# FFN up product by Strassen's scheme, inner activations to DRAM, down product as a phase of its own

## The chip, the cores and the metric

The program runs on one core of one Trainium2 chip. The metric is the device time of one execution in microseconds (us). A core has five engines that run in parallel and each take their own instructions in order: PE (TensorE: matmuls, with PEld its weight loads), DVE (VectorE), ACT (ScalarE), POOL (GpSimd) and SP, whose queue starts most of the transfers (DMA). Matmul results land in PSUM, everything else lies in SBUF.

## What is computed

The kernel does one step of a two-layer decoder for 1024 prompt positions and 64 sample positions (8 batches of 8), 1088 tokens in all, with a width of 1024. Each layer mixes the positions and then applies a feed-forward block with a causal convolution of three taps, and each of the two is followed by a normalisation of the residual sum:

```python
def conv_ffn(x, buf, w_up, conv_w, conv_b, w_down):
    h = x @ w_up                                   # 1024 -> 2 * 2816
    h, new_buf = causal_dwconv(h, buf, conv_w, conv_b)
    return (jax.nn.silu(h[..., :D_FF]) * h[..., D_FF:]) @ w_down, new_buf
...
x = layer_norm(ALPHA * x + mix, ...)
y, buf = conv_ffn(x, ...)
x = layer_norm(ALPHA * x + y, ...)
```

Only the feed-forward block, called FFN here, is changed. It runs twice, once per layer.

## The kernel before

Products are made nearly in float32: every operand is split into a high part and the rest (`split`, line 211: ACT rounds a copy, DVE subtracts it from the original), and `mm3` (line 202) makes three matmuls, high by high, high by low and low by high, for each product.

**The FFN** (`ffn`, line 255). The 2 x 2816 inner rows are taken in 22 blocks of 128 + 128 rows (gate and value). `up(blk)` loads and splits both weight blocks (`load_split`, 512 KB each) and goes through the tokens in three tiles of 364 columns; for each tile and half it makes 8 x 3 matmuls into one PSUM bank. ACT applies the middle tap (line 298), DVE adds the other two taps straight from PSUM (line 302), ACT applies SiLU, DVE multiplies (line 317) and the result is split again into `act`. `down(blks)` multiplies two blocks' activations by their rows of the down weights, 9 token tiles by two halves of 512 columns, and DVE adds each PSUM bank to the residual `res` in SBUF (line 352). `ffn` runs the up product two blocks ahead of the down product, so that PE has both kinds of work in turn. POOL has two small copies per block (lines 308, 314).

**Around it.** `out_ln` (line 1366) makes the residual sum and normalises it tile by tile; `to_T` (line 241) transposes each tile on PE and splits it into `x_`, which `ffn` reads. After the last `down` the loop `ffn_ln` (line 380) normalises the nine tiles while the last products run. In layer 0 the projection `in1` (line 1450) follows, in layer 1 the program ends. `run` (line 2201) calls them in turn.

**Storage and order.** SBUF is cut into fields A to G (`epoch`, `upper`); a field changes its type as a whole, and only when everything in it is done. Outside the attention stages the order on each engine is made by a scheduler when the program is built; at run time every engine keeps that order, and an instruction that waits holds up those behind it. In the traces the scheduled instructions have the line of the helper that records them.

Of the kernel before, what the change touches and what calls it, by code (L numbers as in the profile page):

```python
# [15 lines left out]
ALU = mybir.AluOpType  # L16
# [15 lines left out]
FIELDS = dict(A=8704, B=8704, C=9216, D=8768, F=8368)  # L32
TILES = ((0, 364), (364, 362), (726, 362))

# [37 lines left out]
class Group:  # L72
    """storage that is given back together"""
# [4 lines left out]
    def __call__(self, field, *shape):  # L78
        n = math.prod(shape)
        m = (n + 1) // 2 * 2  # L80
        top, field = field[-1] == "^", field.rstrip("^")
        field = next((f for f in field if f in self.net.arenas and self.net.arenas[f].fits(m)), field[0])
# [20 lines left out]
class Halves(tuple):  # L103
    """high and low parts; both: the two as one"""


class Net:
    token_tiles = (8, 0, 1, 2, 3, 4, 5, 6, 7)

    def __init__(self, ctx, tc, A):  # L110
# [7 lines left out]
        for f, t in zip("ABCDF", (F32R, F32R, F32, F32, F32)):  # L118
            self.epoch(f, t)
# [12 lines left out]
    # ---- storage: fields of SBUF, each of one type at a time, and banks of PSUM by use  # L132
# [8 lines left out]
    def upper(self, **fields):  # L141
        """cut the uppermost storage into these fields"""
# [52 lines left out]
    def stack(self, v, rows):  # L195
        """v [128, 2, 4, (hi, lo)]: both parts of the sample group side by side, for each row block"""
# [5 lines left out]
    def mm3(self, out, wh, wl, xh, xl, first, last):  # L202
        mm = self.nc.tensor.matmul
        mm(out, wh, xh, start=first, stop=False)  # L204
        mm(out, wh, xl, start=False, stop=False)  # L205
        mm(out, wl, xh, start=False, stop=last)  # L206
# [8 lines left out]
    def load_split(self, hi, lo, raw, src, eng=None):  # L215
        """src (DRAM, float32) by way of raw as its high and low parts"""
# [24 lines left out]
    def to_T(self, x, M, x_, c0):  # L241
        """x [M, 128 k] -> columns c0.. of the high and low parts x_: for each four k their [128, k, .]"""
# [11 lines left out]
    # ---- the feed-forward block: res <- ALPHA res + ffn(x)  # L254
    def ffn(self, i, x_, res):
        nc, A = self.nc, self.A
        g = self.group()
        raws = [g("F", D) for _ in range(4)]
        cpar = g("F", 2 * NBLK, 4)
        nc.sync.dma_start(cpar, A["ffn_cp"][i])  # L260
        stt = g("F", 2 * NBLK, NB, 2)
        nc.sync.dma_start(stt, A["ffn_st"][i])
        ffp = g("F", 2 * NBLK, 2)
        wu = [g("EG", 2, D) for _ in range(2)]
        wd = [g("EG", 2, D) for _ in range(2)]
        # a block's rows of all tokens: high parts, low parts of the sample group, of the prompt
        act = [g("D", 2 * NT) for _ in range(4)]
        high, low = (lambda a, c0, c1: a[:, c0:c1]), (lambda a, c0, c1: a[:, NT + NS + c0 : NT + NS + c1])
        nc.gpsimd.memset(res[NS:, NTT - 1, :], 0.0)
        cc = [g("F", 2, 364) for _ in range(2)]  # L270
        pr_ = g("F", D)
        pr = [pr_[:, 364 * k : 364 * k + 364] for k in range(2)]
        hh = [g("F", NB, 10) for _ in range(2)]
        cnt = dict(c=0, h=0)

        def up(blk):
            ws = []
            for half in range(2):
                w = wu[half]
                self.load_split(w[:, 0, :], w[:, 1, :], raws[half], A["w_up"][i, half * NBLK + blk])  # L280
                ws.append(w.rearrange("p s (k c) -> p s k c", k=8))
            a = act[blk % 4]
            for n in range(3):
                c0 = (0, 362, 724)[n]
                c, prod = cc[cnt["c"] % 2], pr[cnt["c"] % 2]
                cnt["c"] += 1
                wid = 364 if n == 0 else 362
                o0 = 364 - wid
                np_ = 298 if n == 2 else wid
                for half in range(2):  # L290
                    cb = half * NBLK + blk
                    w = ws[half]
                    ps = self.ps("mm")[:, :364]
                    for k in range(8):
                        xh, xl = (v[:, k % 4, c0 : c0 + 364] for v in x_[k // 4])
                        self.mm3(ps, w[:, 0, k, :], w[:, 1, k, :], xh, xl, k == 0, k == 7)
                    o = c[:, half, :]
                    nc.scalar.activation(o[:, :wid], ps[:, o0:], AF.Identity, bias=cpar[:, cb, 3:4], scale=cpar[:, cb, 2:3])  # L298
                    for tap, sh in ((1, 1), (0, 2)):
                        lo_ = max(0, sh - o0)  # L300
                        s0 = lo_ + o0 - sh
                        nc.vector.scalar_tensor_tensor(  # L302
                            o[:, lo_:np_], ps[:, s0 : s0 + np_ - lo_], cpar[:, cb, tap : tap + 1], o[:, lo_:np_], op0=ALU.mult, op1=ALU.add
                        )
                    if n == 2:
                        h = hh[cnt["h"] % 2]
                        cnt["h"] += 1
                        nc.gpsimd.tensor_copy(h[:, :, 0:2], stt[:, cb])
                        nc.scalar.copy(h[:, :, 2:10], ps[:, 300:].rearrange("p (b t) -> p b t", b=NB))
                        nc.scalar.copy(ffp[:, cb, :], ps[:, 298:300])  # L310
                        os = o[:, 298:362].rearrange("p (b t) -> p b t", b=NB)
                        for tap in (1, 0):
                            nc.vector.scalar_tensor_tensor(os, h[:, :, tap : tap + 8], cpar[:, cb, tap : tap + 1], os, op0=ALU.mult, op1=ALU.add)
                        nc.gpsimd.tensor_copy(stt[:, cb], h[:, :, 8:10])  # L314
                nc.scalar.activation(c[:, 0, :wid], c[:, 0, :wid], AF.Silu)
                t0 = (0, 364, 726)[n]
                nc.vector.tensor_tensor(prod[:, :wid], c[:, 0, :wid], c[:, 1, :wid], op=ALU.mult)
                nc.scalar.copy(a[:, t0 : t0 + wid], prod[:, :wid])
                if n < 2:
                    self.lo(low(a, t0, t0 + wid), prod[:, :wid], a[:, t0 : t0 + wid])  # L320
                else:
                    self.lo(low(a, t0, LP), prod[:, : LP - t0], a[:, t0:LP])
                    self.lo(a[:, NT : NT + NS], prod[:, LP - t0 : wid], a[:, LP:NT])

        def down(blks):
            ws = []
            for n, blk in enumerate(blks):
                # the last blocks take the place of the other weights
                w = (wd + wu)[n if len(blks) > 2 else blk % 2]
                self.load_split(w[:, 0, :], w[:, 1, :], raws[2 + blk % 2], A["w_dn"][i, blk])  # L330
                ws.append(w)
            def product(tt, pss, q):
                a_, b_ = tt * P, tt * P + P
                for nh in range(2):
                    cs, ps = slice(nh * 512, nh * 512 + 512), pss[nh]
                    for j in range(q, q + 2):
                        a, w = act[blks[j] % 4], ws[j]
                        first, last = j == 0, j == len(blks) - 1
                        if tt < 8:
                            self.mm3(ps, high(a, a_, b_), low(a, a_, b_), w[:, 0, cs], w[:, 1, cs], first, last)  # L340
                            continue
                        # both parts of the sample group at once, on 64 partitions each
                        for s in range(2):
                            nc.tensor.matmul(ps, a[:, LP : NT + NS], w[:, s, cs], start=first and s == 0, stop=last and s == 1)  # L344

            def add(tt, pss):
                for nh in range(2):
                    o = res[:, tt, nh * 512 : nh * 512 + 512]
                    if blks[0] == 0:
                        nc.vector.scalar_tensor_tensor(o, o, ALPHA, pss[nh], op0=ALU.mult, op1=ALU.add)  # L350
                    else:
# [1942 lines left out]
```

## Time and profile before

| | us |
|---|---|
| three runs | 3164.09, 3173.86, 3179.25 (median 3173.86) |
| span of the profiled execution, first to last instruction | 3159.4 |
| PE busy in the span | 3094.1 (98%) |
| DVE busy | 2127.2 (67%) |
| ACT busy | 1360.8 (43%) |
| POOL busy | 766.9 (24%) |

The profile gives no other time of its execution than the span. The difference between the span and the runs, 4.7 us for the fastest and 14.5 for the median, is what lies around it and how runs differ. A matmul's own duration in the rows is longer than the distance to the next one, since matmuls overlap; what one costs is read from the distance between starts.

### The profile page before, as it was taken

Reading aid. Unit: us, or ns where it says so; the run is one execution under the profiler, and the core shown is the slowest. Engines: PE = TensorE matmul, PEld = TensorE weight load, DVE = VectorE, ACT = ScalarE, POOL = GpSimd, SP = SyncE. Lnnn points to the kernel's source line nnn. Section 1 sums busy time; section 2 is a strip of 40 time slices with the busy share of each in tenths; the row PEclk is TensorE's granted clock in tenths of the full one; section 3 lists DMA queues with packets and bytes.
Section 4 is the critical chain, followed back from the end, with each engine's and each line's share of the span. In section 5 each row is a group of like instructions: output and inputs, shape, how many; then the busy total and the mean of one; then the engine's idle time right before and its main releaser. Section 6 shows DMA issues by size and latency. Waiting matters only on the chain.

```text
span 3159.4 us, 47267 instructions
## 1 busy us (share of the span) xinstructions
PE 3094.1 (98%) x18447; PEld 2797.6 (89%) x18447; DVE 2127.2 (67%) x3952; ACT 1360.8 (43%) x2527; POOL 766.9 (24%) x755
## 2 busy tenths in 40 slices
PE   8999999999999999999999999999999999999998
PEld 7888788999999999798998888888789999999997
DVE  8763648555555555747667999999685555555557
ACT  3434533322232232245555888888433222222221
POOL 3652520000000000201112999899200000000000
PEclk9998899999999999999999999999999999999999
DMA  3214131111111111310003444444511111111112
GB/s 138 79 47 122 53 131 56 52 43 41 41 48 46 41 47 43 108 36 23 31 28 103 165 167 156 178 158 167 202 57 41 54 41 41 41 53 42 41 41 75
DMA packets 83026, 243.02 MB, mean 77 GB/s; under 512 B 14908, under 2 KB 36604, under 8 KB 74484
## 3 DMA queue, kind: packets, MB, share of 16 engines
q1 hardware_dynamic: 71504, 154.98, 15.2%
q0 software_dynamic: 9216, 83.89, 7.4%
q8 instruction: 146, 2.39, 0.3%
q10 hardware_dynamic: 2084, 1.14, 0.1%
q14 instruction: 76, 0.62, 0.1%
HBM read 214.11 MB, written 24.68 MB: 76 GB/s over the span
## 4 chain that ended last, share of the span: by engine, by line
PE 82%; DVE 11%; ACT 4%; issue 2%; DMA 1%; POOL 1%; ACTq 0%; DVEq 0%; SPq 0%; POOLq 0%
PE ps L204 22%; PE ps L206 22%; PE ps L205 22%; DVE fieldF L2065 2%; DVE fieldD L209 2%; PE ps L2121 1%; PE ps L2011 1%; PE ps L344 1%; PE ps L2044 1%; DVE fieldF L2087 1%; DVE fieldB L209 1%; PE ps L1800 1%; PE ps L249 1%; PE ps L2025 1%; PE ps L1769 1%
## 5 line engine op out<-in xcount | busy, mean ns | idle before, releaser
L205 PE MATMUL ps<-fieldB,fieldE 128*128 128x364 f32 (+1 forms) x1488 | 494.5, 332 | 0.1
L302 DVE SCALAR_TENSOR_TENSOR fieldF<-ps,fieldF 128x362 f32<-128x362 f32 (+2 forms) x528 | 301.6, 571 | 284.7 <-ACT fieldF L298 275.7
L204 PE MATMUL ps<-fieldA,fieldE 128*128 128x364 f32 (+3 forms) x1440 | 477.0, 332 | 7.7 <-ACT fieldA L725 7.4
L206 PE MATMUL ps<-fieldA,fieldE 128*128 128x364 f32 (+3 forms) x1440 | 477.5, 332 | 0.0
L204 PE MATMUL ps<-fieldB,fieldE 128*128 128x364 f32 (+1 forms) x1104 | 365.4, 331 | 0.0
L206 PE MATMUL ps<-fieldB,fieldE 128*128 128x364 f32 (+1 forms) x1104 | 364.0, 330 | 0.0
L314 POOL COPY fieldF<-fieldF 128x16 f32<-128x16 f32 x88 | 17.4, 198 | 1399.9 <-ACT fieldF L310 1348.0
L205 PE MATMUL ps<-fieldA,fieldE 128*128 128x364 f32 x1056 | 347.2, 329 | 0.0
L352 DVE TENSOR_TENSOR fieldC<-fieldC,ps 128x512 f32<-128x512 f32 x324 | 222.2, 686 | 165.8 <-PE ps L206 163.6
L205 PEld LDWEIGHTS ps<-fieldB,fieldE 128*128 128x128 f32 x1488 | 283.8, 191 | 1.3 <-DVE fieldB L726 0.5
L204 PEld LDWEIGHTS ps<-fieldA,fieldE 128*128 128x128 f32 x1440 | 273.6, 190 | 9.9 <-ACT fieldA L725 7.4
L206 PEld LDWEIGHTS ps<-fieldA,fieldE 128*128 128x128 f32 x1440 | 273.8, 190 | 2.1 <-issue 0.9
L298 ACT ACTIVATE fieldF<-ps,fieldF 128x362 f32<-128x362 f32 (+1 forms) x264 | 172.5, 653 | 200.4 <-PE ps L206 200.4
L218 ACT CAST fieldE<-fieldF 128x1024 fp32r<-128x1024 f32 (+2 forms) x144 | 136.5, 958 | 280.9 <-PE ps L206 170.9
L219 DVE TENSOR_TENSOR fieldE<-fieldF,fieldE 128x1024 fp32r<-128x1024 f32 (+1 forms) x140 | 156.4, 1127 | 92.8 <-ACT fieldE L218 77.5
L204 PEld LDWEIGHTS ps<-fieldB,fieldE 128*128 128x128 f32 x1104 | 208.7, 189 | 0.9 <-issue 0.7
L206 PEld LDWEIGHTS ps<-fieldB,fieldE 128*128 128x128 f32 x1104 | 208.3, 189 | 0.1
L205 PEld LDWEIGHTS ps<-fieldA,fieldE 128*128 128x128 f32 x1056 | 198.6, 188 | 1.7
L204 PE MATMUL ps<-fieldE,fieldD 128*128 128x512 f32 (+1 forms) x480 | 187.4, 391 | 0.0
L205 PE MATMUL ps<-fieldE,fieldD 128*128 128x512 f32 (+1 forms) x480 | 185.6, 387 | 0.0
L206 PE MATMUL ps<-fieldE,fieldD 128*128 128x512 f32 (+1 forms) x480 | 185.4, 387 | 0.0
L209 DVE TENSOR_TENSOR fieldD<-ps,fieldE 128x1024 fp32r<-128x1024 f32 x128 | 153.9, 1209 | 0.6 <-ACT fieldE L2015 0.4
(596 smaller groups left out, 7289.3 us busy)
## 6 DMA issues: line engine op xcount, KB each, us to landing
fieldF<-w_up SPq DMA_DIRECT2D x88, 512.0 KB, 3.5
fieldF<-w_dn SPq DMA_DIRECT2D x44, 512.0 KB, 4.0
fieldF<-w_in SPq DMA_DIRECT2D x16, 512.0 KB, 4.0
fieldF<-w_out SPq DMA_DIRECT2D x32, 256.0 KB, 2.9
fieldC<-x_T SPq DMA_DIRECT2D x8, 544.0 KB, 7.0
fieldC<-x_tok SPq DMA_DIRECT2D x8, 512.0 KB, 6.3
xs<-fieldC SPq DMA_DIRECT2D x8, 512.0 KB, 2.6
Od<-fieldF SPq DMA_DIRECT2D x32, 128.0 KB, 1.7
```

The costliest lines, as they stand in the source:

```text
L204: mm(out, wh, xh, start=first, stop=False)
L205: mm(out, wh, xl, start=False, stop=False)
L206: mm(out, wl, xh, start=False, stop=last)
L209: self.nc.vector.tensor_tensor(out, full, hi, op=ALU.subtract)
L218: self.nc.scalar.copy(hi, raw)
L219: (eng or self.nc.vector).tensor_tensor(lo, raw, hi, op=ALU.subtract)
L249: nc.tensor.transpose(t[:, j * M : (j + 1) * M], x[:, (a + j) * P : (a + j + 1) * P], self.ident[:M, :M])
L298: nc.scalar.activation(o[:, :wid], ps[:, o0:], AF.Identity, bias=cpar[:, cb, 3:4], scale=cpar[:, cb, 2:3])
L302: nc.vector.scalar_tensor_tensor(o[:, lo_:np_], ps[:, s0 : s0 + np_ - lo_], cpar[:, cb, tap : tap + 1], o[:, lo_:np_], op0=ALU.mult, op1=A ...
L344: nc.tensor.matmul(ps, a[:, LP : NT + NS], w[:, s, cs], start=first and s == 0, stop=last and s == 1)
L352: nc.vector.tensor_tensor(o, o, pss[nh], op=ALU.add)
L2065: V.tensor_tensor_reduce(o, ps[H], o, op0=ALU.add, op1=ALU.max, accum_out=out[H], scale=1.0, scalar=first)
```

## The change

The rewritten `ffn` does three things.

**Strassen's scheme.** Weights and tokens are cut in halves: the weights' four blocks are the two halves of the contraction by gate and value rows, and the tokens are handled in two parts `u` of 544, each cut into 2 x 2 blocks of 512 contraction rows by 272 tokens. Instead of eight block products there are seven, P1 to P7 (`PRODUCTS`), each 4 x 3 matmuls with 272 columns. Their left factors are A11, A12, A22 and four sums S1 to S4 of weight blocks, made by POOL for every block of 128 rows (`sums`, and S4 in `weights`); their right factors are made once per FFN (`tokens`) and stay in fields A to E. Three of the products are added onto the PSUM bank of another. `taken` adds the products up into `R`, in SBUF; `conv` applies the taps from there, SiLU on ACT, the multiplication now on POOL.

**Activations to DRAM.** `conv` writes each block's product of gate and value to `actd` in DRAM, four DMAs per block.

**A down phase.** After all 22 blocks the tokens are taken in three groups of three tiles; for each, all 22 blocks of activations and down weights are loaded, split and multiplied, and the sums stay in six PSUM banks until the group ends. The residual comes from DRAM (`xm`, written by `out_ln`). The down weights are loaded three times. Normalisation of one group runs beside the next group's products; the last three blocks of the last group are done tile by tile.

```diff
+PRODUCTS = dict(P1=("A11", "B11"), P6=("S2", "T2"), P2=("A12", "B21"), P5=("S1", "T1"), P7=("S3", "T3"), P4=("A22", "T4"), P3=("S4", "B22"))
...
+        def tokens(u):
...
+            def parts(p, full, eng=V):
+                nc.scalar.copy(X[p][u][:, 0], full)
+                sub(eng, X[p][u][:, 1], full, X[p][u][:, 0])
+            parts("P1", B11)
+            parts("P2", B21)
+            sub(V, B11, B12, B11)
+            sub(G, B12, B22, B12)
+            parts("P3", B22, G)
+            sub(V, B22, B22, B11)
+            sub(V, B21, B21, B22)
+            parts("P6", B22)
+            parts("P5", B11)
+            parts("P7", B12, G)
+            parts("P4", B21)
...
+            G.tensor_tensor(S[0], A11, A21, op=ALU.subtract)
+            G.tensor_tensor(A21, A21, A22, op=ALU.add)
+            G.tensor_tensor(S[1], A21, A11, op=ALU.subtract)
...
+        def weights(p):
+            self.split(*W[p], self.left[PRODUCTS[p][0]])
+            if p == "P1":
+                G.tensor_tensor(self.left["S4"], self.left["A12"], self.left["S2"], op=ALU.subtract)
...
+            on = dict(P2="P1", P7="P6", P3="P5").get(p)
+            ps = bank[on or p, u]
+            x = X[p][u]
+            for k in range(4):
+                wh, wl = (w[:, k * P : k * P + P] for w in W[p])
+                self.mm3(ps, wh, wl, x[:, 0, k], x[:, 1, k], k == 0 and not on, k == 3, skip_group_check=on is not None)
...
+            if p == "P1":
+                nc.scalar.copy(s1, bank["P1", u])
+            elif p == "P2":
+                nc.scalar.copy(g_[:, h1], bank["P1", u])
+            elif p == "P6":
+                add(U2, s1, bank["P6", u])
+            elif p == "P7":
+                add(U3, s1, bank["P6", u])
+                add(v_[:, h2], U3, bank["P5", u])
+            elif p == "P4":
+                add(v_[:, h1], U3, bank["P4", u])
+            elif p == "P3":
+                add(g_[:, h2], U2, bank["P5", u])
...
+                nc.scalar.activation(y, x[:, 2:], AF.Identity, bias=c(3), scale=c(2))
+                for tap in (1, 0):
+                    V.scalar_tensor_tensor(y[:, :n], x[:, tap : tap + n], c(tap), y[:, :n], op0=ALU.mult, op1=ALU.add)
...
+            nc.scalar.activation(a, a, AF.Silu)
+            G.tensor_tensor(a, a, b, op=ALU.mult)
...
+                nc.sync.dma_start(d[:, at : at + c1 - c0], a[:, c0:c1])
...
+            for p in PRODUCTS if blk else first:
+                for u in range(2) if blk else (1,):
+                    product(p, u)
+                for u in range(2) if blk else (1,):
+                    taken(p, u)
+                if blk + 1 < NBLK:
+                    weights(p)
...
+            for u in range(2):
+                conv(blk, u)
...
+            nc.sync.dma_start(raw, actd[k][:, c0 : c0 + N])
+            self.load_split(w[:, 0], w[:, 1], wr[n % 2], A["w_dn"][i, k])
...
+        fetch(0, 0)
+        fetch(0, 1)
+        for u in range(2):
+            conv(NBLK - 1, u)
...
+            if n + 2 < len(todo):
+                fetch(*todo[n + 2])
...
+            for j in range(3):
+                product2(b, k, j)
```

`out_ln` writes each normalised tile to DRAM and `to_raw` leaves its transpose unsplit. `in1` keeps two buffers for its raw weights where it had four, and field F is now two fields, F and H.

**Places in the order of the instructions.** In rows of the order, `field...` are the SBUF fields, `ps...` the PSUM banks, then the columns.

DVE in the middle of an FFN, before (line 317 the product of gate and value, 209 and 219 splits, 302 taps read from PSUM, 313 taps of the sample group):

```order
L317 TENSOR_TENSOR fieldF5_67<-fieldF5_67 128x362
L209 TENSOR_TENSOR fieldD10_3695<-fieldF5_67,fieldD10_3695 128x362
L219 TENSOR_TENSOR fieldE7_71<-fieldF5_67,fieldE7_71 128x1024
L302 SCALAR_TENSOR_TENSOR fieldF5_67<-ps410_7346,fieldF5_67 128x298 x2
L313 SCALAR_TENSOR_TENSOR fieldF5_67<-fieldF5_67 128x64 x2
```

The same engine in the change, where one block ends and the next begins (380 and 390 are the taps of `conv`, 216 the weights' splits, 358 the additions in `taken`; the two rows with ps350 and ps351 take up P6 of the next block):

```order
L380 SCALAR_TENSOR_TENSOR fieldA10_2594<-fieldA10_2594,fieldF5_67 128x480
L390 SCALAR_TENSOR_TENSOR fieldA10_2594<-fieldA10_2594,fieldF5_67 128x64 x2
L216 TENSOR_TENSOR fieldH14_3847<-fieldA10_2594,fieldH14_3847 128x512
L390 SCALAR_TENSOR_TENSOR fieldA10_2594<-fieldA10_2594,fieldF5_67 128x64
L358 TENSOR_TENSOR fieldA10_2594<-fieldA10_2594,ps350_6987 128x272
L358 TENSOR_TENSOR fieldA10_2594<-fieldA10_2594,ps351_7000 128x272
L216 TENSOR_TENSOR fieldH14_3847<-fieldF5_67,fieldH14_3847 128x512
L216 TENSOR_TENSOR fieldH14_3847<-fieldA10_2594,fieldH14_3847 128x512 x2
```

The taps read their values from SBUF now, and the last taps of a block stand in front of the first additions of the next.

DVE in the change where `out_ln` ends and the FFN of layer 0 begins (245 and 246 the normalisation of the last tile, 301 the subtractions of `tokens`, 216 the weights' splits):

```order
L245 SCALAR_TENSOR_TENSOR fieldC12_3709<-fieldC12_3709,bmva0_7_4417,fieldF5_67 128x1024
L244 RECIPROCAL brsa0_7_4422<-brsa0_7_4422 128x1
L301 TENSOR_TENSOR fieldE16_4444<-fieldA10_2594,fieldE16_4444 128x1088
L246 SCALAR_TENSOR_TENSOR fieldC12_3709<-fieldC12_3709,brsa0_7_4422,fieldF5_67 128x1024
L216 TENSOR_TENSOR fieldH14_3847<-fieldF5_67,fieldH14_3847 128x512 x2
L216 TENSOR_TENSOR fieldE16_4444<-fieldF5_67,fieldE16_4444 128x512 x2
L301 TENSOR_TENSOR fieldC19_4450<-fieldA10_2594,fieldC19_4450 128x1088 x2
```

The parts of P1, the first product, lie in the new field C and so stand behind the last use of the old one. Thirteen more subtractions of that size follow on DVE, with a few additions between them; before, the first tile's matmuls stood directly behind the last product of `out_ln`.

SP's queue in the change, at the end of the up product (398 the writes of activations, 454 and 224 the loads of the down phase):

```order
L398 DMA act0_4451<-fieldA10_2594 128x256
L398 DMA act0_4451<-fieldA10_2594 128x288
L502 DMA fieldF5_67<-xm0_3711 64x1024
L398 DMA act0_4451<-fieldA10_2594 128x480
L398 DMA act0_4451<-fieldA10_2594 128x64
L454 DMA fieldF5_67<-act0_4451 128x320
L224 DMA fieldF5_67<-w_dn 128x1024
```

The loads of the first three blocks' activations stand ahead of these rows; the fourth block's stand behind the last block's writes.

## Rows read from the trace of the kernel before

**Rows 1.** The page: busy time by engine, and the span in 40 slices.

```profile
PE 3094.1 (98%) x18447; PEld 2797.6 (89%) x18447; DVE 2127.2 (67%) x3952; ACT 1360.8 (43%) x2527; POOL 766.9 (24%) x755
...
PE   8999999999999999999999999999999999999998
```

**Rows 2.** Chain of waits, two down tiles of layer 0: start us, us, what.

```profile
627.41 1.87 PE ps L344 x8
...
1278.37 1.88 PE ps L344 x8
```

**Rows 3.** Timeline of PE, first 364-column matmul of 25 in a row, and the last.

```profile
799.94 0.33 PE L205 MATMUL ps<-fieldB,fieldE 128*128 128x364 f32 x1
...
803.94 0.33 PE L205 MATMUL ps<-fieldB,fieldE 128*128 128x364 f32 x1
```

**Rows 4.** Timeline of PE, first 256-column matmul of ten in a row, and the last.

```profile
1479.20 0.28 PE L206 MATMUL ps<-fieldB 128*128 128x256 f32 x1
...
1480.27 0.28 PE L206 MATMUL ps<-fieldB 128*128 128x256 f32 x1
```

**Rows 5.** Groups by line and shape, DVE: busy us, mean ns | idle before.

```profile
L209 DVE TENSOR_TENSOR fieldB<-ps,fieldB 128x256 fp32r<-128x256 f32 x67 | 26.5, 420 | 22.0 <-ACT fieldB L1736 19.3 <-ACT fieldB L1811 1.8 <-PE ps L2011 0.9
L219 DVE TENSOR_TENSOR fieldE<-fieldF,fieldE 128x512 fp32r<-128x512 f32 x28 | 20.1, 738 | 3.3 <-issue 2.4 <-ACT fieldE L218 0.9
L238 DVE SCALAR_TENSOR_TENSOR fieldC<-fieldC,bmva,fieldF 128x1024 f32<-128x1024 f32 x16 | 20.5, 1279 | 0.4
L313 DVE SCALAR_TENSOR_TENSOR fieldF<-fieldF 128x64 f32<-128x64 f32 x176 | 51.4, 292 | 31.3 <-ACT fieldF L310 28.2
L726 DVE TENSOR_TENSOR fieldB<-fieldC,fieldA 128x1088 fp32r<-128x1088 f32 x8 | 10.3, 1291 | 0.9 <-ACT fieldA L725 0.7
```

**Rows 6.** The same, ACT.

```profile
L218 ACT CAST fieldE<-fieldF 128x512 fp32r<-128x512 f32 x28 | 16.7, 618 | 59.5 <-PE ps L1381 50.8 <-DMA fieldF<-w_out 8.4 <-PE ps L205 0.2
L725 ACT CAST fieldA<-fieldC 128x1088 fp32r<-128x1088 f32 x8 | 8.8, 1103 | 2.5 <-DMA fieldC<-x_T 2.5
L898 ACT COPY fieldD<-ps 128x272 f32<-128x272 f32 x16 | 5.8, 383 | 6.7 <-PE ps L891 6.5
```

**Rows 7.** Single lines of POOL: duration ns min/median/max, first and last start.

```profile
L1240 POOL TENSOR_TENSOR fieldG<-fieldG,fieldA x8: 1036/1045/1047, 329.3 to 408.6; 128x512 f32<-128x512 f32 x8
L1323 POOL TENSOR_TENSOR fieldD<-fieldD x4: 2488/2514/2703, 370.9 to 422.1; 128x1088 f32<-128x1088 f32 x4
L314 POOL COPY fieldF<-fieldF x88: 197/198/200, 555.1 to 3104.2; 128x16 f32<-128x16 f32 x88
```

**Rows 8.** One DVE line over all its runs, in the form of rows 7.

```profile
L2087 DVE SCALAR_TENSOR_TENSOR fieldF<-fieldF x64: 205/1298/2014, 1743.8 to 2242.6; 64x1 f32<-64x1 f32 x64
```

**Rows 9.** Timelines of DVE and of POOL around one of them.

```profile
1910.98 1.68 DVE L2087 SCALAR_TENSOR_TENSOR fieldF<-fieldF 64x1 f32<-64x1 f32 x1
...
1910.27 2.38 POOL L1997 TENSOR_TENSOR fieldB<-fieldA,fieldB 128x1024 fp32r<-128x1024 f32 x1
```

**Rows 10.** Timeline of PE where the first FFN follows `out_ln`.

```profile
529.16 0.39 PE L206 MATMUL ps<-fieldG,fieldD 128*128 128x512 f32 x1
529.39 0.33 PE L204 MATMUL ps<-fieldA,fieldE 128*128 128x364 f32 x1
```

**Rows 11.** Stretches after layer 0's FFN: busy us of PE, PEld, DVE, ACT, POOL, granted clock, DMA share, GB/s.

```profile
1330.00:1332.00 2.00, 0.00 (x0) 0.00 (x0) 2.00 (x3) 1.33 (x2) 2.00 (x1) 1.00 0.79 184
...
1334.00:1336.00 2.00, 1.17 (x5) 0.81 (x4) 0.69 (x1) 1.08 (x3) 2.00 (x2) 0.50 0.52 196
...
1344.00:1346.00 2.00, 2.00 (x17) 2.00 (x16) 1.72 (x3) 1.17 (x2) 0.00 (x0) 1.00 0.46 152
```

**Rows 12.** The end: the last matmul, and the last work of DVE.

```profile
3149.30 0.39 PE L206 MATMUL ps<-fieldE,fieldD 128*128 128x512 f32 x1
...
3154.59 1.28 DVE L239 SCALAR_TENSOR_TENSOR fieldC<-fieldC,brsf,fieldF 128x1024 f32<-128x1024 f32 x1
```

**Rows 13.** The page, DMA issues: KB each, us from issue to landing.

```profile
fieldF<-w_dn SPq DMA_DIRECT2D x44, 512.0 KB, 4.0
```

More of the change, by code (lines that the diff above doesn't have):

```diff
@@ L264, in ffn @@
[L264 to L274, printed above, removed]
@@ L325, in down @@
[L325 to L351, printed above, removed]
-                        nc.vector.tensor_tensor(o, o, pss[nh], op=ALU.add)
-            n = 2 if len(blks) > 2 else 0
-            some = {tt: [self.ps(("ac", "mm")[k]) for _ in range(2)] for k, tt in enumerate(self.token_tiles[:n])}
-            for tt, pss in some.items():
-                product(tt, pss, 0)
-            for tt in self.token_tiles:
-                pss = some.get(tt) or [self.ps("ac") for _ in range(2)]
-                for q in range(2 if tt in some else 0, len(blks), 2):
-                    product(tt, pss, q)
-                add(tt, pss)
@@ new lines, in load, with sums @@
+        def load(blk):
+            raw = raws[blk % len(raws)]
+            for half in range(2):
+                nc.sync.dma_start(raw[:, half * D : half * D + D], A["w_up"][i, half * NBLK + blk])
+        def sums(blk):
+            raw = raws[blk % len(raws)]
+            A11, A12, A21, A22 = (raw[:, k * 512 : k * 512 + 512] for k in range(4))
+            G.tensor_tensor(S[0], A11, A21, op=ALU.subtract)
+            G.tensor_tensor(A21, A21, A22, op=ALU.add)
+            G.tensor_tensor(S[1], A21, A11, op=ALU.subtract)
+            self.left = dict(A11=A11, A12=A12, A22=A22, S1=A21, S2=S[1], S3=S[0], S4=A11)
@@ new lines, in ffn @@
+        first = ("P1", "P2", "P6", "P5", "P7", "P4", "P3")
+        load(0)
+        sums(0)
+        for p in first:
+            weights(p)
+        tokens(0)
+        gt[0].free()
+        xf = "AD"[i]
+        R = [[gr(xf, 2 + HT) for _ in range(2)] for _ in range(2)]
+        U = [[gr(xf, QT) for _ in range(3)] for _ in range(2)]
+        hh = [gr(xf, NB, 2 + LS) for _ in range(2)]
+        for half in range(2):
+            G.memset(R[0][half][:, :2], 0.0)
+        for p in first:
+            product(p, 0)
+            taken(p, 0)
@@ new lines, in ffn @@
+        tokens(1)
+        gt[1].free()
+        o = [gr(xf, 2, HT) for _ in range(2)]
+        raws.append(gr(xf, 2 * D))
+        for blk in range(NBLK):
+            if blk + 1 < NBLK:
+                load(blk + 1)
+                sums(blk + 1)
+            for p in PRODUCTS if blk else first:
[3 more added lines that the diff above has]
+                    taken(p, u)
+                if blk + 1 < NBLK:
+                    weights(p)
+            if blk + 1 == NBLK:
+                break
+            for u in range(2):
+                conv(blk, u)
@@ L390, in ffn_ln @@
+        gl.free()
+        yield
+        for j in range(3):
+            for k in range(NBLK - 3, NBLK):
+                product2(2, k, j)
+            finish(2, j)
+        for j in range(3):
+            norm(2, j)
+            if j == 2:
+                g.free()
             yield
-        g.free()
 def lay(a):
@@ L1065, in ssd_decay @@
         gt.free()
-        rows = [bf(self.gd("F", 544), NT) for _ in range(2)]
+        rows = [bf(self.gd("HF", 544), NT) for _ in range(2)]
         for k, v in enumerate((cs, ec)):
@@ L1363, in mix0, with out_ln @@
         return [self.m0, m1]
-    def out_ln(self, name, i, m_, x_, res, src, ks=range(8), rows=None):
+    def out_ln(self, name, i, m_, XT, res, src, dst, ks=range(8), rows=None):
         nc, A = self.nc, self.A
@@ L1454, in in1 @@
         g = self.group()
-        raws = [g("F", 2, 352) for _ in range(4)]
+        gw = self.group()
+        raws = [gw("F", 2, 352) for _ in range(2)]
         ws = []
@@ L1854, in prompt_attention @@
         ot = [g("F^", 256) for _ in range(2)]
-        pb = [g("F^", LP) for _ in range(4)]
+        pb = [g("H^", LP) for _ in range(4)]
         mneg = g("F^", P)
@@ L2232, in run @@
         self.banks(mm=1, tr=2, ac=1)
-        gm, gt, gr = self.group(), self.group(), self.group()
+        gm, gt, gr, *gd = (self.group() for _ in range(5))
         heads = range(8)
@@ L2257, in run @@
         next(self.sample, None)
-        m_, res, rest = out
+        m_, XT, rest = out
         for a in range(2):
@@ L2267, in run @@
             pass
-        self.ffn(1, m_, res)
-        for _ in self.ffn_ln(1, res, A["o_y"]):
+        gm.free()
+        gr.free()
+        ffn = self.ffn(1, XT, gd, xm[1], A["o_y"], "AB")
+        next(ffn)
+        ffn.send(None)
+        for _ in ffn:
             pass
```

291 lines of the change are left out of this document (184 added, 107 removed).

## The prediction

> **What bounds the kernel now.** The page comes first: PE works in 98% of the span, DVE in 67%, ACT in 43%, POOL in 24%, and PE's slices are full from end to end [rows 1]. So the matmuls set the time, and an edit pays if PE issues less without starting to wait. The chain of waits shows the rhythm: the sample tile's eight down matmuls recur from 627.41 to 1278.37 in nine steps, 72.33 us for two FFN blocks [rows 2]. 22 blocks are 796 us, and the two FFNs half of the span. PE's timeline splits a block. From 799.94 to 803.94 lie 24 distances of 364-column matmuls, 166.7 ns each [rows 3]; a block's up product has 3 x 2 x 8 x 3 = 144 of them, **24.0 us**. The down product gets the rest, 36.17 - 24.0 = **12.2 us** for 52 matmuls, 234 ns each, the same as 1.87 us for eight [rows 2]. Last, where the FFN meets its neighbours: the first up matmul follows the last of `out_ln` at once [rows 10]; at the end PE's last matmul starts at 3149.30 and the span lasts 10.1 us more, most of it DVE's [rows 12].
>
> **The up product on PE.** 7 products x 2 parts x 12 = 168 matmuls of 272 columns take the place of 144 of 364. The nearest row is 256 columns: nine distances from 1479.20 to 1480.27, 118.9 ns each [rows 4]. Between it and 166.7 for 364, 272 comes to 126.0 (bounds: 118.9, and 166.7 for no gain from fewer columns). Taken: 126.0, so **21.2 us**. If PE kept that, the change would save 2.8 x 44 blocks = 125 us. The down product keeps its 52 matmuls per block: nothing.
>
> **What DVE and POOL now do per block.** DVE: 7 weight splits x 0.738 = 5.2; eight taps from SBUF, four of 544 and four of 480 columns, between 0.292 for 64 columns and 1.279 for 1024, 0.785 and 0.72, together 6.0; four of 64, 1.2 [rows 5]. These 12.4 us all have two inputs in SBUF. Ten additions from PSUM, 0.42 for 256 columns, some 0.446 for 272, are 4.5 more [rows 5]. DVE has 16.9 us. POOL: four weight sums x 1.045, two products of gate and value x 1.1 (by its 512 columns, scaled), ten small copies x 0.2: 8.4 us [rows 7]. ACT, by 0.618 for a cast of 512 and 0.383 for 272 columns, has 7 casts, 4 copies and 6 passes of 544, near 10 us: hidden under 21.2 [rows 6].
>
> DVE alone would fit as well. But the trace shows that it cannot run freely beside POOL: a DVE instruction on one column per partition, 205 ns at best, takes 1298 in the median and 2014 at most [rows 8], and one that starts at 1910.98 ends at 1912.66, just when POOL's at 1910.27 ends, after 2.38 us [rows 9]. So I add up: 12.4 + 8.4 = 20.8 us exclusive, under 21.2 if the PSUM additions run beside POOL; with nothing beside POOL, 16.9 + 8.4 = 25.3.
>
> The order adds a wait. The last taps of a block stand ahead of the next block's first additions on DVE, and those free the banks of P1 and P6, onto which P7 is summed. After a block's last product DVE has some 7.7 us of its work left before them (three additions, the taps, two splits), with all of POOL's 8.4 in between 16.1. P7 comes four products of two parts, 8 x 1.51 = 12.1 us, into the next block. PE so stalls between 0 and 4.0 us a block. I take 0.5, near the lower end, since POOL's sums are spread over the block: **21.7 us**, or (24.0 - 21.7) x 44 = **-101**.
>
> The Trainium skill has this rule in "SBUF — State Buffer", section "SBUF: two separate sides": the port pair that DVE and GpSimd share is an exclusive lock, and the other "fully blocks" for the whole instruction. By that rule the change trades PE time for a contested port, and its full form is the second rival below; the trace agrees in the stretched instruction of 1.68 us [rows 9].
>
> **The start of each FFN.** The cover is gone here: `tokens` needs all normalised tiles before a product. After the last `out_ln` matmul come the tile's additions and normalisation, near 8 us with two passes of 1.28 and the splits that the order puts between them; transposes and copies, 1.5; a cast, 1.1; the first subtraction, 1.29 [rows 5, 6]: PE idles 12 to 13 us. Then DVE feeds it: 13 more subtractions x 1.29 = 16.8, additions 0.9, and POOL's four of 2.5 [rows 5, 7], 0 to 10 of which cost the port, and 3 us of PE behind the last. Block 0 ends 33.7 to 43.9 us after `out_ln` and has 21.2 of work: 12.5 to 22.7 lost. An idle PE is also granted less: after 1330 the clock fell from 1.00 to 0.50, which is 1.2 GHz, and was 1.00 again by 1344 [rows 11], up to 4 us. Taken: 20 per FFN, **+40** (25 to 54).
>
> **From up to down.** The loads for three blocks stand ahead of the last writes on SP, and carry PE for 3 x 3.7 = 11 us. The fourth's stand behind the last writes, after 8 to 16 us of `conv`, and need a landing, 4.0 us for the 512 KB weights [rows 13], and a split. PE waits 0 to 8; taken 4 per FFN, **+8**. Later each block of the down phase has 3.7 to 4.2 us of PE against one 4.0 us load two blocks ahead, four casts and splits: nothing, and the loads' threefold bytes cost nothing as long as that cover holds.
>
> **The ends.** The last group's tiles are normalised one behind the other: some 13 us after PE against 10.1 [rows 12], +3. `in1` with two raw weight buffers can start its loads later; PE was idle there, at 1330 to 1346, for stretches already [rows 11]: 0 to 5, taken 3. Together **+6**.
>
> **The sum.** -101 + 40 + 8 + 6 = -47. The profiled 3159.4 us become 3112; the median lies 14.5 above that span, so I forecast **3127**.
>
> **The rivals.**
> *Clean gain.* POOL's work falls into DVE's gaps and PE sets the pace at 21.2. For it: 20.8 < 21.2. Starts of 14: -125 + 28 + 4 + 3 = -90, **3084**. Against it: the sum is within 2% of the pace, and the order has taps ahead of P7's banks.
> *The port decides (slower).* POOL's long instructions lie across DVE's chain at the block's end, and P7 waits 2.3 us per block: 23.5. Then -22 + 54 = +32, **3206**. For it: the row where a tenfold stretch is the median [rows 8]; the far end of the sum is 25.3. Against: additions from PSUM are no second SBUF input. It decides from 22.8 us per block, where 44 x 1.2 no longer pays the 54 of starts and ends.
> *The gain is eaten.* Blocks of 22.3 to 22.7 with starts at 25 each leave -75 to -57 against 64: **3160 to 3180**, no change.
> *The change doesn't do what it says.* If a matmul had a floor, as the weight load of 128 columns might give, and 272 columns cost 140 ns, the block would be 23.5 on PE alone: **3206** also. Against it: 118.9 at 256 columns [rows 4], in proportion to 364's.
>
> **How the numbers follow.** Forecast case 0.40 (3095 to 3155); clean 0.24; port 0.19; eaten 0.13; floor 0.04. A measurement can tell about 0.5%, 16 us, from no change: 3158 to 3190. Faster holds the forecast case and the clean one, 0.64; same the eaten one and the lower edge of the port, 0.16; slower the rest, 0.20. The range leaves out the better half of the clean case and the dearer half of the port: 3080 to 3205.
>
> **What would show it.** Distances near 126 ns between 272-column matmuls; blocks of 21.2 to 22 us in the middle of an FFN; splits and taps on DVE longer than 0.74 and 0.79 where POOL runs, and PE's waits, if any, at P7 or at the next block's conversions; 12 to 13 us of idle PE with 0.50 behind it at each FFN's start; a short wait at the fourth block of the down phase. I am wrong if PE waits in every block for DVE by over 1.5 us, if the down phase is paced by loads, or if the starts cost over 30 us each.

## The result, and the profile after

| | us | ratio to before, 95% interval |
|---|---|---|
| before, median of 4 runs | 3174.2 | |
| the change, median of 4 runs (3097.8 to 3106.6) | **3100.8** | 0.977, 0.975 to 0.979 |
| span of its profiled execution | 3097.1 | 62.3 us under the 3159.4 of before |

Faster, as forecast, by more than forecast (3127), and inside the range. The page of the change, busy time by engine, then PE's slices and clock in 40 slices:

```profile
PE 2967.7 (96%) x19503; PEld 2685.6 (87%) x19503; DVE 2370.2 (77%) x4066; ACT 1554.6 (50%) x2733; POOL 1345.9 (43%) x1299
...
PE   8999998799999999999999999999996999999998
...
PEclk9999899899999999999999999999997999999999
```

Against [rows 1], PE has 126 us less work and now three slices inside the span that are not full (the 7th and 8th with 8 and 7, the 31st with 6): the two starts of an FFN. Three stretches of the windows view tell the FFN of layer 0 (us, then busy us of PE, PEld, DVE, ACT, POOL, granted clock, DMA share, GB/s): out_ln's last matmul to the first product, ten blocks in the middle, the down phase.

```profile
529.70:547.80 18.10, 2.32 (x11) 1.60 (x9) 13.09 (x14) 9.53 (x15) 10.80 (x7) 0.57 0.22 66
...
609.80:821.70 211.90, 211.90 (x1683) 211.90 (x1682) 190.18 (x291) 97.55 (x171) 132.47 (x161) 1.00 0.24 77
1033.40:1299.70 266.30, 266.08 (x1204) 220.23 (x1202) 165.42 (x237) 106.83 (x158) 13.34 (x9) 1.00 0.63 199
```

Ten blocks in 211.9 us are **21.2 us a block**, with PE never idle: 126.1 ns per matmul, as interpolated from [rows 3, 4]. The down phase has PE busy all through, so its threefold loads stay hidden. What the change lost lies ahead of the blocks. PE's timeline there (start us, us, line; in brackets the idle time and what ended it):

```profile
529.66 0.39 PE L213 MATMUL ps<-fieldG,fieldD 128*128 128x512 f32 x1
540.30 1.94 PE L267 MATMUL ps<-ident,fieldC 128*128 128x128 f32 x8 [10.25 <-DVE fieldC L246]
547.77 0.60 PE L211 MATMUL ps<-fieldC,fieldH 128*128 128x272 f32 x1 [5.53 <-ACT fieldC L304]
550.50 0.59 PE L212 MATMUL ps<-fieldC,fieldH 128*128 128x272 f32 x1 [2.13 <-DVE fieldC L301]
...
558.57 0.59 PE L211 MATMUL ps<-fieldB,fieldH 128*128 128x272 f32 x1 [3.95 <-ACT fieldB L304]
563.55 0.60 PE L212 MATMUL ps<-fieldB,fieldH 128*128 128x272 f32 x1 [4.38 <-DVE fieldB L301]
```

Where one matmul followed the last of out_ln at once before [rows 10], PE now waits for DVE and ACT. It stands idle for 10.25 us first, and its granted clock goes to the lower level of 0.50, 1.2 GHz: 0.57 in the mean of 529.7 to 547.8 us, 0.51 from there to 570, and 1.00 afterwards (matmuls of 272 columns stand 0.23 us apart before 570 us, 0.126 later). The up product lasts 503.8 us from out_ln's end to its last matmul (504.8 in layer 1); 22 blocks of 21.2 would be 466. The **start costs 37.8 us** in layer 0 and 38.8 in layer 1. DVE and POOL in the middle of it:

```profile
556.42 3.57 DVE L301 TENSOR_TENSOR fieldA<-fieldA 128x1088 f32<-128x1088 f32 x1 [2.37 <-POOL fieldA L301]
559.91 3.58 DVE L301 TENSOR_TENSOR fieldB<-fieldA,fieldB 128x1088 fp32r<-128x1088 f32 x1
563.42 1.28 DVE L301 TENSOR_TENSOR fieldA<-fieldA 128x1088 f32<-128x1088 f32 x1
...
552.93 5.92 POOL L301 TENSOR_TENSOR fieldA<-fieldA 128x1088 f32<-128x1088 f32 x2 [3.63 <-DVE fieldA L301]
558.79 3.55 POOL L301 TENSOR_TENSOR fieldB<-fieldA,fieldB 128x1088 fp32r<-128x1088 f32 x1
```

The engines take turns: DVE's instruction of 556.42 ends at 559.99, 1.1 us after POOL's pair ends at 558.85, and POOL's next, of 2.5 us alone, takes 3.55. This is the exclusive port of [rows 8, 9], at full force. The end is as forecast: last matmul at 3085.56, 11.5 us ahead of the span's end (10.1 in [rows 12]).

One thing was not forecast. The 512-column matmuls of the down product, 234 ns apart before, stand 227 ns apart:

```profile
1296.82 0.39 PE L211 MATMUL ps<-fieldC,fieldE 128*128 128x512 f32 x1
...
1298.63 0.40 PE L213 MATMUL ps<-fieldC,fieldE 128*128 128x512 f32 x1
```

Eight distances in 1.81 us are 226 ns. So do those of out_ln, whose products the change does not touch. 52 x 44 x 7.4 ns is 17 us that no part of the change explains.

### The profile page after: what moved, and what is told of

Read it like the earlier page. It is cut to its first block, busy times and chain, and to the rows that moved or that the text cites. A ratio compares the mean times of both kernels' runs of the same rounds, so it can differ in the third digit from the quotient of the medians.

```text
span 3097.1 us, 51653 instructions
## 1 busy us (share of the span) xinstructions
PE 2967.7 (96%) x19503; PEld 2685.6 (87%) x19503; DVE 2370.2 (77%) x4066; ACT 1554.6 (50%) x2733; POOL 1345.9 (43%) x1299
## 4 chain that ended last, share of the span: by engine, by line
PE 78%; DVE 13%; ACT 4%; DMA 2%; issue 2%; POOL 2%; ACTq 0%; DVEq 0%; SPq 0%; POOLq 0%
PE ps L211 21%; PE ps L213 21%; PE ps L212 21%; DVE fieldH L2221 2%; PE ps L2277 2%; PE ps L2167 2%; DVE fieldD L216 1%; PE ps L2200 1%; PE ps L471 1%; DVE fieldF L2243 1%; DVE fieldB L216 1%; PE ps L1956 1%; PE ps L2181 1%; PE ps L1925 1%; PE ps L1922 1%
## 5 line engine op out<-in xcount | busy, mean ns | idle before, releaser
L212 PE MATMUL ps<-fieldB,fieldE 128*128 128x272 f32 (+4 forms) x960 | 301.1, 314 | 0.1
L211 PE MATMUL ps<-fieldC,fieldE 128*128 128x512 f32 (+2 forms) x740 | 286.3, 387 | 0.0
L213 PE MATMUL ps<-fieldC,fieldE 128*128 128x512 f32 (+2 forms) x740 | 285.9, 386 | 0.0
L212 PE MATMUL ps<-fieldC,fieldE 128*128 128x512 f32 (+2 forms) x740 | 285.7, 386 | 0.0
L216 DVE TENSOR_TENSOR fieldE<-fieldF,fieldE 128x512 fp32r<-128x512 f32 (+4 forms) x265 | 157.1, 608 | 110.7 <-ACT fieldE L456 103.4
L226 DVE TENSOR_TENSOR fieldC<-fieldF,fieldC 128x1024 fp32r<-128x1024 f32 x132 | 162.3, 1230 | 100.5 <-ACT fieldC L225 100.1
L211 PE MATMUL ps<-fieldC,fieldH 128*128 128x272 f32 x704 | 206.5, 293 | 11.8 <-ACT fieldC L304 11.7
L212 PE MATMUL ps<-fieldC,fieldH 128*128 128x272 f32 x704 | 205.0, 291 | 4.9 <-DVE fieldC L301 4.9
L213 PE MATMUL ps<-fieldC,fieldH 128*128 128x272 f32 x704 | 205.3, 292 | 0.0
L211 PE MATMUL ps<-fieldA,fieldE 128*128 128x362 f32 (+4 forms) x560 | 180.7, 324 | 7.6 <-ACT fieldA L878 7.3
L212 PEld LDWEIGHTS ps<-fieldB,fieldE 128*128 128x128 f32 x960 | 185.4, 193 | 2.0 <-DVE fieldB L879 0.5
L213 PE MATMUL ps<-fieldA,fieldE 128*128 128x362 f32 (+4 forms) x560 | 182.0, 325 | 0.0
L211 PE MATMUL ps<-fieldB,fieldE 128*128 128x272 f32 (+2 forms) x576 | 171.7, 299 | 2.5 <-DVE fieldD L358 2.5
L213 PE MATMUL ps<-fieldB,fieldE 128*128 128x272 f32 (+2 forms) x576 | 170.6, 296 | 0.0
L213 PEld LDWEIGHTS ps<-fieldC,fieldE 128*128 128x128 f32 x740 | 138.9, 188 | 28.2 <-DVE fieldE L216 0.4
L212 PEld LDWEIGHTS ps<-fieldC,fieldE 128*128 128x128 f32 x740 | 138.8, 188 | 27.4
L211 PEld LDWEIGHTS ps<-fieldC,fieldE 128*128 128x128 f32 x740 | 139.0, 188 | 26.9
L380 DVE SCALAR_TENSOR_TENSOR fieldA<-fieldA,fieldF 128x544 f32<-128x544 f32 (+1 forms) x176 | 145.8, 866 | 21.4 <-ACT fieldA L378 21.4
```

The costliest lines, as they stand in the source:

```text
L211: mm(out, wh, xh, start=first, stop=False, **kw)
L212: mm(out, wh, xl, start=False, stop=False, **kw)
L213: mm(out, wl, xh, start=False, stop=last, **kw)
L216: self.nc.vector.tensor_tensor(out, full, hi, op=ALU.subtract)
L226: (eng or self.nc.vector).tensor_tensor(lo, raw, hi, op=ALU.subtract)
L380: V.scalar_tensor_tensor(y[:, :n], x[:, tap : tap + n], c(tap), y[:, :n], op0=ALU.mult, op1=ALU.add)
```

## The experiments

In the profiled executions of all these kernels out_ln ends between 529 and 540 us, before the work that the edits of the change are about; so stretches are compared from there on where a few us matter. One FFN is taken from the last out_ln matmul to the first of `in1` in layer 0, to the end in layer 1; its up product ends with the last 272-column matmul.

| kernel | ratio to before | FFN 0, us | FFN 1, us | up product 0 / 1, us |
|---|---|---|---|---|
| before | 1 | 799.9 | 807.9 | |
| e1 before, fields moved | 0.991 (0.989 to 0.993) | 786.1 | 794.6 | |
| the change | 0.977 (0.975 to 0.979) | 770.0 | 775.5 | 503.8 / 504.8 |
| e2 down weights 32 bytes on | 0.982 (0.980 to 0.984) | 778.2 | 781.6 | 505.1 / 503.4 |
| e3 early fields | 0.977 (0.974 to 0.979) | 767.2 | 771.0 | 500.2 / 499.2 |
| e4 POOL + 4 sums | 0.997 (0.996 to 0.999) | 800.9 | 806.8 | 534.8 / 534.7 |
| e5 tokens on DVE | 0.976 (0.974 to 0.977) | 761.9 | 767.3 | 496.1 / 496.6 |
| e6 all on DVE, early fields | **0.970** (0.968 to 0.972) | 756.1 | 760.8 | 489.1 / 489.0 |
| e7 POOL + 2 sums, not block 0 | 0.981 (0.979 to 0.983) | 771.7 | 777.5 | 505.8 / 506.8 |
| e8 all on DVE, late fields | **0.970** (0.968 to 0.972) | 756.3 | 760.3 | 490.6 / 489.6 |

**The 7 ns: e1 and e2.** The change cuts field F in two and makes D smaller. That moves fields E and G: in before E starts at 196384 bytes of a partition and G 16384 further on, both 32 behind a multiple of 64; in the change E starts at 196480, a multiple of 128. e1 is the kernel before with E and G at the places of the change; e2 is the change with its down weights shifted by 8 elements, 32 bytes.

```diff
-FIELDS = dict(A=8704, B=8704, C=9216, D=8768, F=8368)
+FIELDS = dict(A=8704, B=8704, C=9216, D=8768, F=8392)
```
```diff
+        g("C", 8)
         wd = [g("C", 2, D) for _ in range(4)]
```

> The kernel before with field F 24 elements longer, so that fields E and G start on a multiple of 64 bytes in SBUF (as in the change), where they started 32 bytes behind one. In the trace of the change a 512-column matmul costs 227 ns, in that of before 234, in stages that the change doesn't touch too. Theory start address: the 7 ns are one more line of 64 bytes (16 columns at 2.4 GHz, 6.7 ns) that a 2048-byte row of the moving operand touches when it starts off the boundary. Then 2288 down matmuls and 832 of the output projections, which read their moving operand from E or G, fall from 234 to 227 ns: 3120 x 7.4 = 23 us, about 3136 us in the profiled span, ratio 0.993. Rival: the 7 ns belong to the order of the changed program (groups of three on a bank, other engines); then the distances stay at 234 and the ratio at 1.000.

> The change with eight unused elements ahead of the down weights in field C, so that their rows start 32 bytes behind a multiple of 64. Theory start address: the 2288 down matmuls take 234 ns where they took 227, + 17 us, about 3118 us, ratio 0.982 to 0.983 where the change had 0.977. Rival (order of the program): 227 ns, 3101 us, 0.977.

e1, PE's timeline, the first and last of 13 matmuls of 512 columns and of 38 of 364:

```profile
789.73 0.39 PE L205 MATMUL ps<-fieldG,fieldD 128*128 128x512 f32 x1
...
792.45 0.39 PE L205 MATMUL ps<-fieldG,fieldD 128*128 128x512 f32 x1
```
```profile
599.74 0.33 PE L204 MATMUL ps<-fieldB,fieldE 128*128 128x364 f32 x1
...
605.79 0.33 PE L205 MATMUL ps<-fieldA,fieldE 128*128 128x364 f32 x1
```

and e2, the first and last of 18 of 512 columns:

```profile
1159.84 0.39 PE L211 MATMUL ps<-fieldC,fieldE 128*128 128x512 f32 x1
...
1163.80 0.40 PE L213 MATMUL ps<-fieldC,fieldE 128*128 128x512 f32 x1
```

12 distances in 2.72 us are 227 ns in e1, 17 in 3.96 are 233 in e2: the time follows the address, in either program, and not the order.

The 364-column matmuls of e1, whose stationary operand lies in E, fell as well (37 distances in 6.05 us are 163.5 ns), which I had not expected; but not all of them. The first and last matmul of the first token tile of a block in e1, and of the second:

```profile
612.00 0.33 PE L204 MATMUL ps<-fieldA,fieldE 128*128 128x364 f32 x1
...
619.83 0.33 PE L206 MATMUL ps<-fieldB,fieldE 128*128 128x364 f32 x1
620.00 0.32 PE L204 MATMUL ps<-fieldA,fieldE 128*128 128x364 f32 x1
...
627.67 0.33 PE L206 MATMUL ps<-fieldB,fieldE 128*128 128x364 f32 x1
```

47 distances each, 166.6 and 163.2 ns. In before the three tiles took about 167, 166.6 and 165.7 ns, in e1 166.5, 163.3 and 163.5. So the first tile hardly gained. The weights lie at the same place for all three, the moving operand doesn't (it starts at columns 0, 362 and 724), so its place seems to count too; no run varied it alone.

e1 gained 29 us where 23 were expected, 13.8 and 13.3 of them in the FFNs. e2 lost 17.6 us by the medians and 14.3 in its two FFNs, where 17 were expected. So the kernel before can have 27 us in its FFNs by addresses alone, without Strassen, where the change gained 62 there; against e1 the change stands at 0.977 / 0.991 = 0.986.

**Which addresses: e9 to e12**, one run each, with 16, 4, 32 and 64 unused elements where e2 has 8. Compared is the down product's stretch in the trace, not the whole time.

> The change with sixteen unused elements (64 bytes) ahead of the down weights in field C, where eight (32 bytes) had cost 7 ns per matmul. Theory line of 64 bytes: the rows start on a boundary again, 227 ns, span about 3097 us. Rival (any shift of the field, or the unused elements themselves): 234 ns, about 3116 us.

> The same with four unused elements (16 bytes). Theory line of 64 bytes: a row of 2048 bytes touches 33 lines instead of 32 whatever the offset, 234 ns, span about 3115 us. Rival (the cost grows with the offset): 230 ns, about 3106 us; or (only halves of a line count) 227 ns, 3097 us.

> The change with 32 unused elements (128 bytes) ahead of the down weights. The line of 64 bytes is not what decides: 16, 32 and 64 bytes gave 232, 234 and 229 ns, and no shift 227. Theory period of 128 bytes: 227 ns, down product 266 us in layer 0. Rival (a longer period): 228 to 234 ns, 267 to 273 us.

> The same with 64 unused elements (256 bytes). Theory period of 128 or of 256 bytes: 227 ns, 266 us. Rival (a longer period, or the place relative to the stationary operand in field E): 228 ns or more, 267 us or more.

17 distances in a row in e11, then in e12:

```profile
1159.67 0.39 PE L211 MATMUL ps<-fieldC,fieldE 128*128 128x512 f32 x1
...
1163.63 0.40 PE L213 MATMUL ps<-fieldC,fieldE 128*128 128x512 f32 x1
```
```profile
1166.21 0.39 PE L212 MATMUL ps<-fieldC,fieldE 128*128 128x512 f32 x1
...
1170.06 0.39 PE L211 MATMUL ps<-fieldC,fieldE 128*128 128x512 f32 x1
```

They are 233 and 226 ns. Down product of layer 0, from the up product's last matmul to the first of `in1`: no shift 266.2 us (265.8 to 267.0 in e3 to e8, which don't shift it either), 16 bytes 271.2, 32 bytes 273.1, 64 bytes 268.4, 128 bytes 272.1, 256 bytes 266.1. The line of 64 bytes, my mechanism, falls with the 64 and the 128, and so does a period of 128. A period of 256 bytes fits all six. In the fast cases with 512 columns (the change, e1, e12) both operands start 128 bytes behind a multiple of 256. Whether that place counts, or only that both have the same one, these runs don't tell. Neither carries over to 364 columns: in the first token tile of e1 both operands start there too (fields A and B, which hold the tokens, start at 16512 and 51328), and it is the slowest of the three tiles. The mechanism stays open.

**The start: e3, e5, e6, e8.** e3 exchanges fields so that P1's parts needn't wait for C (the part of the line that changes):

```diff
-("P1", gc, "C"), ("P6", gc, "C"), ("P2", ge, "E"), *((p, gx, fields) for p in ("P5", "P7", "P4", "P3"))
+("P7", gc, "C"), ("P4", gc, "C"), ("P2", ge, "E"), *((p, gx, fields) for p in ("P1", "P6", "P5", "P3"))
```

> The change with the places of the token parts exchanged: those of P1 and P6 in the field that is free with the last product of out_ln (B in layer 0, A in layer 1), those of P7 and P4, which come last, in field C, which has to wait for the normalised tile's write. Theory wait for C: the first product starts some 5 us after the last out_ln product where it started 18 us after it, and PE's loss at each FFN's start falls from 37 us by 10: 3081 us, ratio 0.971. Rival: 22 subtractions on DVE and POOL, stretched by each other, feed PE anyway, and the wait for C runs beside them: less than 5 us in all, ratio 0.976 or more.

The first product did start at once, 0.2 us after out_ln's last where it had been 18. But PE then stood 11.7 us for the last tile's normalisation, which now shares DVE with the first subtractions:

```profile
552.13 1.94 PE L267 MATMUL ps<-ident,fieldC 128*128 128x128 f32 x8 [11.66 <-DVE fieldC L246]
```

The up product ended 4 to 6 us earlier per FFN, and the whole time fell by 2 us: the rival, nearly. The wait for C was not what cost most; it ran beside work that PE would have waited for anyway.

e5 moves the six subtractions of `tokens` from POOL to DVE (`sub(G, ...)` and two `parts(..., G)`):

> The change with the six subtractions that tokens gives POOL (three per part u) on DVE instead. Theory port at the start: from out_ln's last product to the end of the subtractions DVE and POOL take turns on one port; rows there are 3.6 us where 1.28 is the work. Six times 2.5 us of POOL leave that queue and six times 1.2 of DVE join it, -7 us per FFN: the loss at each start falls from 37 to 30 us, about 3085 us, ratio 0.972. Rival (DVE alone feeds PE, POOL's six ran beside it): + 7 us per FFN, about 3115 us, ratio 0.982.

Two of DVE's subtractions in e5:

```profile
563.10 1.29 DVE L301 TENSOR_TENSOR fieldA<-fieldA 128x1088 f32<-128x1088 f32 x1
564.30 1.29 DVE L301 TENSOR_TENSOR fieldB<-fieldA,fieldB 128x1088 fp32r<-128x1088 f32 x1
```

Minus 7.7 and 8.2 us in the up products, though DVE has more to do: the subtractions that stood at 3.6 us are 1.29 now. The port was the cost, with DVE's wait for POOL's results (2.37 us in the rows of the change) as a smaller part that the run doesn't separate. e6 has both edits and the four weight sums on DVE as well (`G.tensor_tensor` to `V.tensor_tensor`, four places); e8 is e6 without the fields' exchange.

> Three edits together: the token parts placed as in the run with early fields, the six token subtractions on DVE, and POOL's four weight sums per block on DVE too. POOL keeps the product of gate and value and the small copies. Theory port: in the middle of an FFN nothing changes (DVE's 16.9 us with four sums of 0.6 to 0.74 stay under 21.2, blocks of 21.2 us); at the start POOL's sums no longer stretch DVE's chain, and with the port gone the early fields begin to pay: loss 20 to 25 us where it was 37, 3070 to 3080 us, ratio 0.967 to 0.970. Rival (DVE becomes the bound of the block): blocks of 21.5 us or more, no gain over the change, 0.977 or higher.

> The run with all three edits, but with the token parts back in their places of the change (P1 and P6 in field C). It parts the 15 us per FFN that the three edits gained. Theory early fields pay once the port is free: with P1 behind field C again the first product starts some 17 us after out_ln's last, and of the 15 us at least 5 are lost: up product 494 us or more from out_ln's end, about 3085 us, ratio 0.973. Rival (DVE's chain alone sets the start, as it did with the early fields alone): within 2 us per FFN of the three edits, 3074 to 3078 us, ratio 0.970.

e6 takes 15 us off each up product; e8 shows, against what I had expected, that the fields have no part in it (up products within 1.5 us). In the middle of an FFN the same edit makes DVE's splits shorter and the block no faster. Groups of DVE from 700 to 800 us, the change and e6:

```profile
L216 DVE TENSOR_TENSOR fieldH<-fieldF,fieldH 128x512 fp32r<-128x512 f32 x11 | 11.9, 1095 | 0.4 <-ACT fieldH L219 0.4
```
```profile
L216 DVE TENSOR_TENSOR fieldH<-fieldF,fieldH 128x512 fp32r<-128x512 f32 x10 | 6.7, 681 | 2.8 <-ACT fieldH L219 2.8
```

1095 ns beside POOL's sums, 681 without: a stretch that PE never sees. e6 and e8, at 0.970, beat both kernels; e8 is the smaller edit. Of the start some 23 us are left in either, with DVE busy in nearly all of it (42.4 of the 44.6 us from out_ln's end at 537.4 to 582 in e6).

**The port in the middle: e4 and e7**, S4 made five times and three times (in e7 not for block 0):

> The change with the weight sum S4 made five times instead of once per block on POOL (the same values): 4 x 1.045 = 4.2 us more POOL work a block. Theory port decides by the sum: 12.4 us of two-input DVE work and 8.4 + 4.2 of POOL make 25.0 us a block, over PE's 21.2: blocks of some 25 us, + 3.8 x 42 = 160 us, ratio 1.027. Rival, slack: what DVE and POOL do to each other is taken up while PE works on; DVE's 19.0 and POOL's 13.3 us a block grow but stay under 21.2: 3101 to 3110 us, ratio up to 0.980.

> The change with S4 made three times instead of once, in all blocks but the first (2.1 us more POOL work per block, the starts as they were). With four extra sums blocks were 22.2 us: start distances on DVE (0.60 for a split, 0.70 and 0.62 for taps) make 10.3 us of two-input work a block, with POOL's 8.4 18.7, with 4.2 more 22.9. Theory port decides by that sum: 20.8 us, under PE's 21.2, so blocks stay at 21.2 us and the time within 3 us of the change, ratio 0.977 to 0.978. Rival (each us of POOL costs its share of 1.0 / 4.2 from the first on): blocks of 21.7 us, + 21 us, ratio 0.984.

The windows view from 700 to 800 us of the change, of e7 and of e4, columns as above:

```profile
700.00:800.00 100.00, 100.00 (x796) 100.00 (x795) 89.06 (x137) 44.97 (x80) 62.93 (x76) 1.00 0.23 74
```
```profile
700.00:800.00 100.00, 100.00 (x796) 100.00 (x795) 93.66 (x140) 46.32 (x82) 75.86 (x84) 1.00 0.26 82
```
```profile
700.00:800.00 100.00, 96.34 (x756) 95.24 (x755) 95.97 (x134) 43.94 (x79) 91.66 (x90) 1.00 0.23 74
```

With 2.1 us more of POOL a block nothing changes on PE, 796 matmuls in either; with 4.2 it stands 3.7% of the time, and blocks take 22.2 us (14 of them from 718.5 to 1029.0). So the port does decide from a point on, as the second rival had it, and not in proportion. Of e4's 65 us about 42 are 1.0 us a block; of the rest some 9 are the later first products, 24.0 and 21.5 us after out_ln, not 18. Its blocks were not the 25 us expected: durations in rows overlap the next instruction's by some 0.08 us, so the sum was too large. By distances between starts (0.60 for a split, 0.70 and 0.62 for the taps, 0.2 for the short ones) DVE has 10.3 us of two-input work, with POOL's 8.4 18.7 a block: 2.5 under PE's pace in the change, 0.4 under it in e7 (20.8), 1.7 over it at e4's 22.9, where 22.2 was measured; the sum is an estimate, 3% too high there. POOL alone would fit, with 12.6 us of its own in e4; it is busy in 91.66 of 100 us because its instructions are stretched as well (a sum of 1.045 us takes some 1.46). e7's whole time was 6 us above the change, 4 of them in its up products, where 3 were allowed for. Its ratio of 0.981 lies between the two expectations; the 796 matmuls decide for the first.

## Why the prediction was right, and where not

- **Bound and pace: right.** PE's 126 ns per 272-column matmul was measured to the digit, and the block's 21.2 us with it.
- **The stall of 0.5 us per block: wrong.** It is 0; the 0.5 that was taken, "near the lower end", cost 22 us of forecast gain. The lower end of its own bounds, and the pace of the clean rival, is what came. The sum of row durations, 20.8, made it look tight where the distances leave 2.5 us.
- **The start, 20 us per FFN: mis-sized**, 38 measured, 77 for both where the upper bound was 54. "I am wrong if ... the starts cost over 30 us each" came true, though the time lies in the range. The idle time to the first product was 18 us, not 12 to 13: POOL's work stretched the normalisation's passes (3.27 us for 1.28), and the transposes ran at half clock. The feed by DVE then took 28.6 us (547.75 to 576.36), or 27.3 without the first subtraction, which the prediction counted as idle time: near the upper of its bounds, 17.7 and 27.7, since the port cost nearly its full price. And "3 us of PE behind the last" subtraction were 12: by 570 us PE had made only a quarter of the block's matmuls, by 576.36 some 55%. e5 took 8 and e8 13 to 15 us of the 38 away by freeing the port; the rest stands beside a DVE that is busy nearly throughout, and no run shortened it further.
- **Up to down, 4 us per FFN: nothing.** The first 512-column matmul starts 0.13 us behind the last of 272, and PE is busy in 266.08 of the next 266.30 us, so nothing waited for the fourth block's loads either.
- **Ends, 6 us:** the tail grew by 1.4. `in1`'s two buffers can't be told apart from nothing: from `in1`'s start to the next out_ln's end the change took 1021.9 us for 1022.4, but e1, with the addresses of the change, 1019.4, and e2 to e12, with the same `in1` as the change, 1018.3 to 1025.0.
- **"The down product keeps its 52 matmuls per block: nothing": wrong** by 6 us in layer 0 (799.9 - 22 x 24.0 = 271.9 before, 266.2 now), which the fields' addresses gave (273.1 in e2). The prediction had the cut of field F before it and priced it only as two buffers for `in1`.

Per FFN, in layer 0: 62 us less on the up product's matmuls, 38 more at the start, 6 less in the down product, -30 in all, where -27 was forecast from -51, +20 and +4. So the sum came near by luck, by errors that cancel: the stall (22 us in all), the change of phase (8) and the down product were taken too dear, the two starts 37 us too cheap. Of the 26 us between 3127 and 3100.8, 15 are of that sum, and 11 the step from span to median: 14.5 us lay between the two for before, whose profiled execution was faster than any of its timed runs, and 3.7 for the change.

Two small slips in the prediction's readings change nothing: a tenfold stretch is the most in [rows 8] (2014 over 205 ns), the median is a sixfold one (1298); and the upper end of block 0 adds up to 43.7 us, not 43.9.

The Trainium skill's rule in "SBUF — State Buffer", section "SBUF: two separate sides", that a DVE instruction with two SBUF inputs or a GpSimd one locks the shared pair for its whole length, is what the start's rows show (3.57 us for 1.28) and what e5 bears out; in the middle of the FFN the splits are stretched too (1095 ns for 681), which costs nothing up to e7's load.

## What to carry to other kernels

Price a contested port by the sum of both engines' exclusive work per period, taken from distances between starts: in this kernel it was free while that sum stayed under the period of the bound engine (18.7 and 20.8 us under 21.2), and paid almost in full at a start with nothing to hide behind, where it was better to give the work to one engine. Look at a phase change not only for the first wait but for how much of the next engine's work is still to do when the feed ends. And where a change moves buffers, compare an untouched stage in both traces first: here 24 unused elements in one field were worth 29 us, and of the 62 us in the two FFNs the change keeps 35 against a kernel before with that edit.

## What was not expected of the hardware

A matmul's pace hung on where its operands start in SBUF: 512 columns at 227 ns with the moving operand 128 bytes behind a multiple of 256, and 229 to 234 when shifted by 16 to 128 bytes; 364 columns between 163.3 and 167 ns, by the place of the stationary one and, as it seems, of the moving one. That is up to 3% of a matmul, and shows in no wait.
